# Two key parts side by side, and score pairs at other distances, in the recurrent half of a hybrid trunk

## The chip, the cores and the metric

The kernel runs on one core of a Trainium2 chip. The time is the device time of that core in microseconds (us). One of the executions is also recorded by the hardware profiler, and its record is what is called the trace here. The engines are named as in the profile: PE is TensorE (PEld its weight loads), DVE is VectorE, ACT is ScalarE, POOL is GpSimd, and SP issues transfers. L1702 is line 1702 of the kernel.

## The reference

The model is a trunk of two layers over 640 tokens (512 latent tokens and 128 context tokens) of width 1024. Layer 0 is gated attention. Layer 1 is a gated linear recurrence with 8 heads of key width 128 and value width 128, which runs over the tokens in both directions. The change touches layer 1 alone. Cut to what matters, it computes:

```python
q, f_fw, f_bw, i_in, g = split(h @ w_in)           # 5 projections of 1024 columns
q = silu(q);  v = i_in                             # per head: 128 keys, 128 values
for d in (fw, bw):
    forget = lb + (1 - lb) * sigmoid(f_d)          # the decay of one token, per key
    k      = (1 - lb) * sigmoid(-f_d)
    S_t = forget_t * S_{t-1} + k_t (outer) v_t     # from s0; backwards for bw
    o_d[t] = q_t @ S_t
o = rms_norm(o_fw + o_bw) * gain * silu(g)
out = o @ w_out                                    # then residual and layer norm
```

The outputs are both token streams, the attention's new keys and values, and the last states of the context tokens.

## The kernel before, in words

**Stages.** The attention layer and the norm behind it come first and are ordered by a planner of their own; the change leaves them alone. Then the recurrent layer goes head by head. For each head `proj_gen` computes the projections (heads 1 to 6 use a scheme of seven products for the two forget projections) and evacuates them into two tiles: `A`, which holds four parts of NT = 640 columns, and `T`, which holds the decays. The four parts of `A` are the forward keys (KF), the backward keys (KB) and the queries times their decays in either direction (QF, QB). `gla_gen` then does the recurrence of the head. All weights and activations of the projections are kept as a high and a low part, so each product is three matmuls; in the profile one line has one of the three.

**The recurrence as levels.** Inside chunks of 128 tokens the recurrence is computed as a matrix of scores. Level 0 takes neighbouring tokens, and level n takes neighbouring blocks of 2^n tokens; level 6 is the last. Each level consists of scores on PE (`scores`, L1666 to L1679) and a step `decay` (L1691): the keys of `A` are multiplied by the decays of their block (L1697 on DVE), ACT copies the keys for the next level into a tile in the right order (`kcopy`, L1647, into a tile with the tag kc or on), the decays are multiplied pairwise (L1701), and the queries of `A` are multiplied (L1702). In heads 0 to 6 the levels 1 to 6 go in pairs: both levels' keys and queries are made ready, with a copy of the queries for the lower level too (`qcopy`, L1652), and then the scores of both are asked for together. Scores are merged by DVE into one tile (L1664), or copied by ACT (L1717) and POOL (L1711). Behind the levels come `kp`, transposes of the keys (L1759) with a copy `kt` (L1761), `sp`, the products for the states of the chunks (L1765, with six updates on DVE at L1768 and L1771, two copies and two stores of the last states), `op`, the outputs (L1782 to L1785, with the sums of squares at L1790, the product with the gate at L1794 and the norm at L1797), and `oT`, their transposes (L1802). The tile of the outputs before these transposes has the tag on, the same as that of some key copies, and there is one buffer for it.

**What sets the order.** Every engine takes its instructions in one order, fixed at compile time. The program is written in an order of asking, and an instruction that has all that it needs by the compiler's own estimate can be put ahead of one asked for earlier. The order of asking is made by a small planner, `Lane` (L102). While the projections of head h + 1 are issued, each piece of them advances the lane's clock by its length in planner's units (1.28 for half a token tile of the value and gate projection, 1.6 for a group of twelve matmuls of the others). `gla_gen` of head h gives a gap with each `yield`, and its next stage is issued at the first piece at which that gap has passed (a stage that is late passes on at most SLIP = 1.0 less). A head's recurrence begins to be issued in the next projection and ends in the one behind that; a negative gap (L1798) lets the next head's recurrence be issued before this one's last stage. `lane.finish(n)` issues all that is left of the oldest heads until n are left. The projection calls it ahead of tiles that need the buffers of earlier heads (L1386, L1541). Tile dependencies, buffers and PSUM banks are held by the framework, which makes an instruction wait for those that read or write what it touches.

**The end.** Head 7 has no pairs. Its levels are issued between pieces of the output projection, whose matmuls have the name `outp`. `gate1` at L1938 takes a buffer of the tag A.

The gaps, as before:

```python
D_GLA = 5.5    # from the first key copy to level 0
D_LEV = 2.7    # a level; a pair takes 2 * D_LEV; one more ahead of kp
D_KT = 2.0     # from kp to sp
D_ST = 3.0     # from sp to op
D_OUT = 7.5    # from op to oT
```

Of the kernel before, what the change touches and what calls it, by code (L numbers as in the profile page):

```python
# [23 lines left out]
NT = TT * P  # L24
# [4 lines left out]
RH = 8  # L29
# [22 lines left out]
FORMS_AT = 3  # L52
D_GLA = 5.5
D_LEV = 2.7
D_KT = 2.0
D_ST = 3.0
D_OUT = 7.5
# [6 lines left out]
def view(t, off, dims):  # L64
    base = t[:]
    return bass.AP(base.tensor, base.offset + off, [list(base.ap[0])] + [list(d) for d in dims])
# [82 lines left out]
def hybrid_step(ctx: ExitStack, tc: tile.TileContext, a: dict, o: dict):  # L149
# [13 lines left out]
    def bank2(name, tag="b2"):  # L163
        return pools["b2"].tile([P, 2, 512], F32, tag=tag if split_banks else "b2", name=name)
# [168 lines left out]
    def gate_load(layer, eng):  # L333
        for s in range(2):
            eng.dma_start(gate[layer][:, s, :], gated[layer][s:s + 1, :].to_broadcast((P, D)))
# [981 lines left out]
            f = slice(4 * nh, 4 * nh + 4)  # L1317
            split_act(h1hi[:, f, t], h1lo[:, f, t], h[:].rearrange("p (a b) -> p a b", a=4))

    KF, QB, QF, KB = 0, NT, 2 * NT, 3 * NT  # L1320

    def wide(ps):
        return ps[:].rearrange("p a b -> p (a b)")
# [236 lines left out]
    lane = Lane()  # L1560
# [75 lines left out]
    def gla_gen(h, H):  # L1636
# [7 lines left out]
        def kcopy(w, tag="kc"):  # L1644
            nb = NT // (2 * w)
            kc = g1.tile([P, NT], F32, tag=tag, name="kc")
            nc.scalar.copy(view(kc, 0, [[2 * w, nb], [w, 2], [1, w]]), view(A, KF, [[2 * w, nb], [KB - KF + w, 2], [1, w]]))  # L1647
            return kc

        def qcopy(w):  # L1650
            nb = NT // (2 * w)
            nc.scalar.copy(view(At, 0, [[2 * w, nb], [w, 2], [1, w]]), view(A, QB, [[2 * w, nb], [QF - QB + w, 2], [1, w]]))  # L1652
            return At
# [9 lines left out]
        def merge(i, pt):  # L1663
            nc.vector.copy_predicated(blocks(near[:], 32), view(masks, i * 32, [[0, TT], [1, 32]]), blocks(pt[:, :32 * TT], 32))  # L1664

        def scores(pt, lev, kc, qc):  # L1666
            w = 1 << lev
            for c in range(TT):
                if lev < 5:
                    for b in range(4):  # L1670
                        t0 = c * P + 32 * b
                        q = qc[:, t0:t0 + 32] if qc else view(A, QB + t0, [[2 * w, 16 // w], [QF - QB + w, 2], [1, w]])
                        mm = nc.tensor.matmul(pt[32 * b:32 * b + 32, 32 * c:32 * c + 32], kc[:, t0:t0 + 32], q, start=True, stop=True)
                else:
                    for b in range(P // w):
                        ko, qo = (KB, QB) if b % 2 else (KF, QF)
                        s0, t0 = c * P + w * b, c * P + w * (b ^ 1)
                        k, q = (kc, qc) if qc else (A[:, ko:ko + NT], A[:, qo:qo + NT])
                        mm = nc.tensor.matmul(pt[w * b:w * b + w, w * c:w * c + w], k[:, s0:s0 + w], q[:, t0:t0 + w],  # L1679
                                              start=True, stop=True)  # L1680
            return mm.ins
# [9 lines left out]
        def decay(lev, keys, query=False):  # L1691
            nonlocal cur, nxt
            w = 1 << lev
            nb = NT // (2 * w)
            kc = qc = None
            kv = view(A, KF, [[KB - KF + w, 2], [2 * w, nb], [1, w]])
            nc.vector.tensor_tensor(kv, kv, view(cur, 1, [[2 * nb - 1, 2], [2, nb], [0, w]]), ALU.mult)  # L1697
            if keys:
                kc = kcopy(2 * w, keys)
            qv = view(A, QB, [[QF - QB + w, 2], [2 * w, nb], [1, w]])  # L1700
            nc.vector.tensor_tensor(view(nxt, 0, [[1, 2 * nb]]), view(cur, 0, [[2, 2 * nb]]), view(cur, 1, [[2, 2 * nb]]), ALU.mult)  # L1701
            last = nc.vector.tensor_tensor(qv, qv, view(cur, 2 * nb + 1, [[-2 * nb - 1, 2], [2, nb], [0, w]]), ALU.mult)  # L1702
            if query:
                qc = qcopy(2 * w)
            cur, nxt = nxt, cur
            return kc, qc, last

        def spread():
            for b in range(4):
                r = slice(32 * b, 32 * b + 32)  # L1710
                nc.gpsimd.tensor_copy(blocks(At[r, :], P)[:, :, r], blocks(near[r, :], 32))  # L1711

        def place(lev, pt):
            w = 1 << lev
            for b in range(P // w):
                r, o_ = slice(w * b, w * b + w), slice(w * (b ^ 1), w * (b ^ 1) + w)
                nc.scalar.copy(blocks(At[r, :], P)[:, :, o_], blocks(pt[r, :w * TT], w))  # L1717

        pairs = h < RH - 1
# [5 lines left out]
        merge(0, pt[:, 512:])  # L1725
        if pairs:
            for lev in (1, 3, 5):
                k2, _, _ = decay(lev, "on" if lev < 5 else None)
                yield 2 * D_LEV
                pt = wide(bank2("lv"))  # L1730
                late = scores(pt[:, 512:], lev + 1, k2, None)
                with tc.issue_after(late):
                    scores(pt, lev, k1, q1)
                k1, q1, last = decay(lev + 1, "kc" if lev < 5 else None, lev < 5)
                if lev < 5:
                    merge(lev, pt)
                    merge(lev + 1, pt[:, 512:])
                else:
                    spread()
                    place(5, pt)  # L1740
                    place(6, pt[:, 512:])
        else:
            for lev in range(1, 7):
                yield D_LEV
                pt = wide(bank2("lv"))
                scores(pt, lev, k1, None)
                k1, _, last = decay(lev, "kc" if lev < 4 else None)
                if lev < 5:
                    merge(lev, pt)
                else:  # L1750
                    place(lev, pt)
                if lev == 4:
                    spread()
        residual.compute(last.ins)
        yield D_LEV
        kp = bank2("kp")
        srcs = [KF + c * P for c in (0, 1, 2, 4)] + [KB + c * P for c in (1, 2, 3, 4)]
        for i, c in enumerate(srcs):
# [2 lines left out]
        nc.scalar.copy(kt, wide(kp))  # L1761
        yield D_KT
        sp = bank2("sp")
# [117 lines left out]
    for h in range(RH):  # L1881
        H = {} if h else H
        if h == RH - 1:
            sxs.close()
            side = reload_gen()
            next(side, None)
        for n, dt in enumerate(proj_gen(h, H, False) if h else first):
            lane.advance(dt)
            if h or n >= FORMS_AT:
                next(side, None)  # L1890
            if h == 0 and n == RES_AT:
                residual.compute()
                residual.loads()
        lane.add(gla_gen(h, H))
# [19 lines left out]
    def tail_steps():  # L1914
# [18 lines left out]
        for ks in ((0,), (1,), (2,), (3, 4, 5), (6,)):  # L1933
            for k in ks:
                out_k(2, k)
            yield

    gate[1] = g2.tile([P, 2, D], F32, tag="A", name="gate1")  # L1938
    gate_load(1, nc.gpsimd)
    xp = lpool("xp", 1)  # L1940
# [139 lines left out]
```

## Time and profile before

| what | value |
|---|---|
| runs | 830.49, 831.3 and 834.88 us, median 831.3 |
| profiled execution, and its span | 830.25 us, 828.4 us |
| PE, PEld busy | 793.3 us (96%), 700.5 us (85%) |
| DVE, ACT, POOL busy | 601.0 us (73%), 446.8 us (54%), 204.1 us (25%) |
| transfers | 98.12 MB, mean 118 GB/s |

Times in the trace count from the start of the span. The recurrent layer's heads with the seven products repeat with a period of about 46.5 us (L1794 of head 2 stands at 518.26, of head 3 at 564.65). Matmuls are pipelined, and their ends in the trace are modelled: a matmul normally begins before the one ahead of it has ended by the record. A matmul in full 32-bit form is two instructions. In the lists in order of time, the first two numbers are start and length in us; a bracket at the end of a row holds the idle time of the engine ahead of it and what ended that. In lists of waits the numbers are the total, how often, and the longest.

### The profile page before, as it was taken

To read this page: it belongs to the slowest core of one execution; us is meant where nothing else is said; L and a number is where in the kernel's file an instruction comes from. 1 tells how busy PE (TensorE), PEld (TensorE's weight loads), DVE (VectorE), ACT (ScalarE), POOL (GpSimd) and SP (SyncE) were. 2 spreads that over 40 slices of the span, in tenths; PEclk is the share of its full clock that TensorE was granted. 3 is DMA by queue.
4 is the path that set the end of the run, shared out by engine and by line. 5 is a ranking of instruction groups with operands and counts; after the bars stand their busy time and mean duration, and the time that the engine had idled before them with its cause. 6 is when DMAs were issued, how large, how long until landed. Compare 5 with 4: busy or idle time off the path is not lost.

```text
span 828.4 us, 19262 instructions
## 1 busy us (share of the span) xinstructions
PE 793.3 (96%) x7953; PEld 700.5 (85%) x7953; DVE 601.0 (73%) x1083; ACT 446.8 (54%) x890; POOL 204.1 (25%) x261
## 2 busy tenths in 40 slices
PE   8999999999999899999999999999999999999994
PEld 6789999888888676888998989898989989897774
DVE  4567767675777876776998795968777795868476
ACT  3252554575666775232564756657484756656242
POOL 0124001354344942101501202122212202131121
PEclk9999999999999999999999999999999999999998
DMA  9943244233140152523322342425142434235041
GB/s 326 396 168 136 102 153 154 77 128 129 51 129 26 54 176 82 198 77 94 104 94 66 106 106 69 126 70 120 46 131 66 108 96 144 84 114 169 29 156 76
DMA packets 36631, 98.12 MB, mean 118 GB/s; under 512 B 5297, under 2 KB 12481, under 8 KB 36545
## 3 DMA queue, kind: packets, MB, share of 16 engines
q1 hardware_dynamic: 25872, 78.95, 28.5%
q0 software_dynamic: 4768, 14.18, 6.1%
q10 hardware_dynamic: 5904, 3.78, 1.5%
q8 instruction: 62, 1.02, 0.5%
q14 instruction: 25, 0.20, 0.1%
HBM read 86.06 MB, written 10.83 MB: 117 GB/s over the span
## 4 chain that ended last, share of the span: by engine, by line
PE 56%; DVE 23%; ACT 10%; issue 5%; DMA 3%; POOL 2%; ACTq 0%; SPq 0%; DVEq 0%; POOLq 0%
PE pot L944 4%; PE outp L1207 4%; PE pt L1030 3%; PE outp L1209 3%; PE outp L1208 3%; DVE A L1702 3%; DVE A L1697 3%; PE rps L1445 3%; PE rps L1447 2%; PE rps L1446 2%; PE sc L917 2%; ACT kc L1647 2%; PE acc L562 2%; PE sc L918 2%; PE gps L374 2%
## 5 line engine op out<-in xcount | busy, mean ns | idle before, releaser
L1023 POOL TENSOR_SCALAR p<-p,rc 128x640 f32<-128x640 f32 x64 | 57.1, 898 | 115.3 <-DVE rc L1022 98.1
L1017 ACT ACTIVATE p<-sc,nm 128x640 f32<-128x640 f32 x64 | 51.2, 802 | 25.1 <-DVE nm L1012 15.9
L1647 ACT COPY kc<-A 128x640 f32<-128x640 f32 x47 | 37.5, 799 | 44.8 <-DVE A L1697 29.7
L1012 DVE TENSOR_REDUCE nm<-sc 128x1 f32<-128x640 f32 x64 | 51.7, 816 | 13.0 <-PE sc L918 12.8
L1711 POOL COPY At<-near 32x160 f32<-32x160 f32 x32 | 15.2, 474 | 182.4 <-PE lv L1679 160.6
L1399 PE MATMUL rps<-h1hi,rw 128*128 128x320 f32 x176 | 55.5, 316 | 0.0
L1401 PE MATMUL rps<-h1hi,rw 128*128 128x320 f32 x176 | 54.9, 312 | 0.0
L1400 PE MATMUL rps<-h1lo,rw 128*128 128x320 f32 x176 | 54.4, 309 | 0.0
L1030 PE MATMUL pt<-small,p 128*128 128x128 f32 x320 | 49.2, 279 | 2.4 <-DVE pts L922 1.2
L1377 PE MATMUL vgps<-rw,h1hi 128*128 128x512 f32 x180 | 49.0, 397 | 0.0
L1030 PEld LDWEIGHTS pt<-small,p 128*128 128x128 f32 x320 | 36.7, 141 | 11.0 <-issue 5.7
L917 PE MATMUL sc<-kk,X 128*128 128x320 f32 x128 | 43.3, 347 | 1.4 <-ACT p L1017 1.2
L922 ACT COPY pts<-pt 128x512 f32<-128x512 f32 x64 | 36.1, 590 | 15.3 <-PE pt L1030 15.2
L944 PE MATMUL pot<-pts,vv 128*64 128x256 f32 x320 | 38.3, 384 | 2.1 <-DVE pts L922 2.0
L374 PE MATMUL gps<-hhi,whi 128*128 128x320 f32 x128 | 40.0, 312 | 0.1
L1377 PE MATMUL vgps<-wspare,h1hi 128*128 128x512 f32 x140 | 39.7, 398 | 0.0
L375 PE MATMUL gps<-hlo,whi 128*128 128x320 f32 x128 | 39.6, 309 | 0.0
L376 PE MATMUL gps<-hhi,wlo 128*128 128x320 f32 x128 | 39.5, 309 | 0.0
L918 PE MATMUL sc<-klo,X 128*128 128x320 f32 x128 | 39.2, 315 | 0.0
L1377 PEld LDWEIGHTS vgps<-rw,h1hi 128*128 128x128 f32 x180 | 32.8, 188 | 7.1 <-ACT s L1510 0.4
L207 POOL TENSOR_TENSOR rstdo<-rs_t,mhalf 128x5 f32<-128x5 f32 x8 | 9.7, 1214 | 109.8 <-DVE rs_t L206 109.8
L383 PE MATMUL qmm<-whi,hhi 128*128 128x256 f32 x120 | 35.0, 292 | 0.1
(347 smaller groups left out, 2611.2 us busy)
## 6 DMA issues: line engine op xcount, KB each, us to landing
raw<-in_rec_w_in SPq DMA_DIRECT2D x40, 512.0 KB, 3.8
raw<-in_ada_m SPq DMA_DIRECT2D x16, 512.0 KB, 8.1
raw<-in_attn_w_in SPq DMA_DIRECT2D x16, 512.0 KB, 4.9
raw<-in_ada_s SPq DMA_DIRECT2D x16, 512.0 KB, 3.8
adaraw<-in_ada_c SPq DMA_DIRECT2D x11, 512.0 KB, 5.5
raw<-in_attn_w_out SPq DMA_DIRECT2D x8, 512.0 KB, 3.8
raw<-in_rec_w_out SPq DMA_DIRECT2D x8, 512.0 KB, 3.8
raw<-in_ada_c SPq DMA_DIRECT2D x5, 512.0 KB, 4.7
```

The source lines that it names most:

```text
L374: nc.tensor.matmul(ps[:, :320], w.hi(k)[:, c], hhi[:, k, t], start=(k == 0), stop=False)
L917: nc.tensor.matmul(out, X[:, h, t0:t0 + P], kk[:, c, k0:k1], start=True, stop=False)
L918: nc.tensor.matmul(out, X[:, h, t0:t0 + P], klo[:, c, k0:k1], start=False, stop=True)
L944: nc.tensor.matmul(pot[j * HD:(j + 1) * HD, :CW], vv[:, slot, c * HD:(c + 1) * HD], moving[j], start=first, stop=last)
L1012: nc.vector.tensor_reduce(nm[:, 0:1], sc[:, :, :320], AX.XY, ALU.max, negate=True)
L1023: nc.gpsimd.tensor_scalar(p, p, rs[:, 0:1], 1.0, ALU.mult, ALU.mult)
L1030: nc.tensor.transpose(pt[:, i * 256 + q * P:i * 256 + (q + 1) * P], ps[q][:, (k0 + i) * P:(k0 + i + 1) * P], ident)
L1377: nc.tensor.matmul(out, h1hi[:, k, t], wvg[i][:, k % 4].rearrange("p e n -> p (e n)"), start=(k == 0), stop=(k == KT - 1))
L1399: nc.tensor.matmul(ps[:, j, :320], hi[:, k, :], h1hi[:, k, t], start=(k == 0), stop=False)
L1400: nc.tensor.matmul(ps[:, j, :320], hi[:, k, :], h1lo[:, k, t], start=False, stop=False)
L1401: nc.tensor.matmul(ps[:, j, :320], lo[:, k, :], h1hi[:, k, t], start=False, stop=(k == KT - 1))
L1647: nc.scalar.copy(view(kc, 0, [[2 * w, nb], [w, 2], [1, w]]), view(A, KF, [[2 * w, nb], [KB - KF + w, 2], [1, w]]))
```

## The change

It has five parts, all in the recurrent layer.

1. The four parts of `A` change places: KF, KB, QB, QF at 0, 1, 2 and 3 NT instead of KF, QB, QF, KB. The step from QB to QF stays NT; that from KF to KB goes from 3 NT to NT.
2. The gap ahead of the second and the third pair goes from 5.4 to 6.0 in heads 0 to 5, and stays 5.4 in head 6.
3. Between level 0 and the first pair there are now two gaps, 2.5 and 4.5. Between them the step `decay` of level 1 is issued, which was issued together with level 0, and ahead of it `lane.finish(1)` issues what is left of the head before, which is its output transposes.
4. The gap from the third pair to `kp` goes from 2.7 to 2.0 in heads 0 to 6.
5. Behind the last projection, head 6 is issued up to its negative gap ahead of `gate1`.

```diff
+D_PAIR = 6.0
+D_LAST = 2.0
+D_TAIL = 2.5
+D_FIRST = 4.5
...
-    KF, QB, QF, KB = 0, NT, 2 * NT, 3 * NT
+    KF, KB, QB, QF = 0, NT, 2 * NT, 3 * NT
...
             for lev in (1, 3, 5):
+                if lev == 1:
+                    yield D_TAIL
+                    lane.finish(1)
                 k2, _, _ = decay(lev, "on" if lev < 5 else None)
-                yield 2 * D_LEV
+                yield D_FIRST if lev == 1 else D_PAIR if h < RH - 2 else 2 * D_LEV
                 pt = wide(bank2("lv"))
...
         residual.compute(last.ins)
-        yield D_LEV
+        yield D_LAST if pairs else D_LEV
         kp = bank2("kp")
...
+    while not lane.gens[0][2]:
+        lane.step(lane.gens[0])
     gate[1] = g2.tile([P, 2, D], F32, tag="A", name="gate1")
```

## The prediction

> **What bounds the kernel now.** I read first the busy shares of the page, then a table of stretches, then TensorE's waits, then one head in order of time. The columns of the table are busy microseconds with the number of instructions, the granted clock and the DMA share.
>
> ```profile
> PE 793.3 (96%) x7953; PEld 700.5 (85%) x7953; DVE 601.0 (73%) x1083; ACT 446.8 (54%) x890; POOL 204.1 (25%) x261
> ```
> ```profile
> 0.00:377.00 377.00, 364.16 (x2769) 310.21 (x2770) 261.04 (x515) 193.08 (x395) 111.86 (x120) 1.00 0.41 141
> ...
> 424.00:470.50 46.50, 45.92 (x613) 42.60 (x612) 36.66 (x61) 26.22 (x42) 4.79 (x8) 1.00 0.25 74
> 470.50:517.05 46.55, 45.30 (x609) 41.99 (x609) 35.40 (x60) 29.02 (x59) 10.96 (x18) 1.00 0.36 97
> 517.05:563.44 46.39, 45.16 (x609) 41.85 (x608) 35.18 (x60) 28.78 (x58) 8.50 (x14) 1.00 0.30 90
> ...
> 656.55:703.00 46.45, 45.23 (x608) 41.84 (x608) 35.23 (x60) 28.86 (x65) 10.97 (x18) 1.00 0.44 126
> 703.00:760.00 57.00, 54.91 (x801) 49.77 (x800) 44.02 (x75) 38.10 (x72) 14.23 (x21) 1.00 0.42 134
> ```
> ```profile
> PE lv L1673 <- DVE A L1702: 5.3, 14, 1.5
> PE lv L1679 <- DVE A L1702: 4.5, 6, 1.2
> PE outp L1207 <- ACT ghi L1812: 0.5, 1, 0.5
> ```
>
> The change lies behind 377 us; nothing ahead of that moves. From there to 817 us TensorE sets the time: in the head of 517.05 it is idle 46.39 - 45.16 = 1.23 us, and all its named waits between 424 and 817 us (the last fence: total, times, longest) are 10.3 us, of which 9.8 us are score matmuls `lv` that wait for the query multiply L1702. The head of 517.05 shows them in order of time:
>
> ```profile
> 519.22 0.86 PE L1377 MATMUL vgps<-wspare,h1hi 128*128 128x512 f32 x3
> 520.01 0.63 PE L1673 MATMUL lv<-A,kc 128*32 128x32 f32 x40
> ...
> 525.06 1.07 PE L1377 MATMUL vgps<-rw,h1hi 128*128 128x512 f32 x4
> ...
> 526.44 0.64 PE L1373 MATMUL vgps<-wspare,h1lo 128*128 128x256 f32 x4
> 526.92 1.09 PE L1377 MATMUL vgps<-wspare,h1hi 128*128 128x512 f32 x4
> 528.40 0.52 PE L1673 MATMUL lv<-A,kc 128*32 128x32 f32 x38 [0.39 <-DVE A L1702]
> ...
> 535.22 0.31 PE L1400 MATMUL rps<-h1lo,rw 128*128 128x320 f32 x1
> 535.71 0.53 PE L1673 MATMUL lv<-A,kc 128*32 128x32 f32 x38 [0.18 <-DVE A L1702]
> ...
> 537.66 0.31 PE L1445 MATMUL rps<-h1hi,rw 128*128 128x320 f32 x1
> ...
> 539.28 0.31 PE L1447 MATMUL rps<-h1hi,rw 128*128 128x320 f32 x1
> 540.25 0.80 PE L1679 MATMUL lv<-A 128*64 128x64 f32 x20 [0.66 <-DVE A L1702]
> 540.98 0.50 PE L1679 MATMUL lv<-At,kc 128*32 128x32 f32 x34
> ...
> 547.04 0.31 PE L1447 MATMUL rps<-thi,wspare 128*128 128x320 f32 x1
> 547.19 1.03 PE L1759 MATMUL kp<-small,A 128*128 128x128 f32 x8
> ...
> 549.83 1.95 PE L1765 MATMUL sp<-vg,kt 128*128 128x128 f32 x16
> ```
>
> Three waits a head, one ahead of each pair of levels: 0.39 + 0.18 + 0.66 = 1.23 us, the whole idle time. Their price is more than the brackets say, since a following matmul otherwise starts before the modelled end of the one before. From start to start: `kp` follows the last `rps` by 547.19 - 547.04 = 0.15 us, but pair 2 follows by 0.49 and pair 3 by 0.97, so 0.34 and 0.82 us are lost. Level 0 at 520.01 follows the third of three `vgps` (spaced 0.23, so at 519.68) by 0.33 us; pair 1 follows the fourth (527.61) by 0.79: 0.46 us. Together **1.62 us a head**.
>
> **The change, part by part.** Two paces are needed. Twelve 320-column matmuls, one step of the projection (1.6 in the planner's units), run 537.66 to 539.28 for eleven spacings: 0.147 each, 1.76 us a step. Eight `vgps` matmuls, half a token tile (1.28), run 525.06 to 526.44: 1.38 us.
>
> *Layout.* Key parts become neighbours, and so do query parts. Nothing is computed more or less; only what overlaps what changes. Before, a view over both key parts reaches from 0 to 4 NT and covers the query parts. The trace shows the order that follows:
>
> ```profile
> 525.81 0.83 DVE L1697 TENSOR_TENSOR A<-A,Tb 128x640 f32<-128x640 f32 x1 [0.35 <-ACT At L1652]
> ...
> 526.67 0.73 ACT L1647 COPY kc<-A 128x640 f32<-128x640 f32 x1 [0.41 <-DVE A L1697]
> ...
> 527.43 0.83 DVE L1702 TENSOR_TENSOR A<-A,Tb 128x640 f32<-128x640 f32 x1 [0.19 <-ACT kc L1647]
> ...
> 541.35 0.82 DVE L1697 TENSOR_TENSOR A<-A,T 128x640 f32<-128x640 f32 x1
> ```
> ```profile
> L1702 DVE TENSOR_TENSOR A<-A,T x32: 810/825/936, 431.8 to 774.3; 128x640 f32<-128x640 f32 x32
> ...
> its engine sat idle before it (us, times) until:
>   ACT kc L1647: 6.7, 15
> ```
>
> The query multiply waits for ScalarE's key copy, and the key multiply for the query copy, though neither touches the other's data. With the two ranges apart, the query multiply can follow the key multiply at once: instead of key multiply, 0.73 us copy, query multiply, the chain loses about 0.35 + 0.19 us of idle time ahead of pair 1, and the copy runs beside it. VectorE is off the path except at the three waits, so this part alone is worth what it takes off them: at least 0.19 us of the first, at most all. It also acts in the last head, which has no pairs.
>
> *Distances.* Working the due times through the planner's rule (a stage is asked for at the first yield of the projection at which it is due): level 0 stays behind the 5th yield; pair 1 goes from the 9th to the 10th, pair 2 from the 13th to the 14th, pair 3 from the 16th to the 18th (the 17th in head 6), `kp` from the 18th to the 19th, `sp` from the 19th to the 20th, `op` from the first half tile of the next projection to the third. Pair 1 thus gets 1.38 us more ahead of it against 0.46 lost. From pair 1 to pair 2 lay one half tile and three steps and now lie four steps: 1.76 - 1.38 = 0.38 us more against 0.34. From pair 2 to pair 3 it is four steps for three: 1.76 us more against 0.82. So the distances alone cover all three waits, the middle one narrowly, and there the layout adds to it. I take all three as gone.
>
> In the sum: heads 1 to 5, 5 x 1.62 = 8.1 us. Head 0 (424.00 to 470.50) is idle 46.50 - 45.92 = 0.58 us: 0.6. Head 6 (703 to 760): its pair 1 waits 1.47 us, in the row below, and 1.38 us of distance with the shorter chain covers it: 1.5. Head 7's level 1 waits 0.48 us behind a key copy of this kind (0.82 us); layout alone acts there, between 0 and 0.48: I take 0.3.
>
> ```profile
> 715.48 0.52 PE L1673 MATMUL lv<-A,kc 128*32 128x32 f32 x38 [1.47 <-DVE A L1702]
> ...
> 755.11 0.82 ACT L1647 COPY kc<-A 128x640 f32<-128x640 f32 x1 [1.02 <-DVE A L1697]
> ...
> 756.94 0.26 PE L1673 MATMUL lv<-A,kc 128*32 128x32 f32 x5 [0.48 <-DVE A L1702]
> ```
>
> Gross gain 8.1 + 0.6 + 1.5 + 0.3 = **10.5 us**.
>
> [...]
>
> *What is moved.* Three rows more of the head of 517.05 are needed:
>
> ```profile
> 533.70 1.22 DVE L1411 TENSOR_TENSOR wspare<-raw,wspare 128x1024 fp32r<-128x1024 f32 x1
> ...
> 543.56 0.49 DVE L1458 TENSOR_TENSOR u<-c,rps 128x320 f32<-128x320 f32 x1 [0.45 <-PE rps L1447]
> ...
> 548.26 1.01 ACT L1761 COPY kt<-kp 128x1024 f32<-128x1024 f32 x1 [2.45 <-PE kp L1759]
> ```
>
> `kp` now has one step behind pair 3 instead of the 5.7 us (541.48 to 547.19) of before. Behind the level-6 scores come 0.50 us of level 5 and 1.76 us of products, 2.26 us; in that time VectorE must do the key multiply (0.82 us, 0.3 us behind the end of the scores in the row of 541.35). It fits by 1.1 us unless VectorE has other work in front: 0 to 0.7 us a head. `sp` keeps its one step behind `kp`, against a copy of 1.01 us: nothing. Its six state updates, two copies and two stores on ScalarE's queue follow it and are needed by `op`, which also moves: nothing. `op` comes 2 x 1.38 us later, with its squares, the power on GpSimd, the product with the gate, and the residual's loads and stores on GpSimd's queue (25% busy). The output transposes stay behind the 7th half tile, so their slack shrinks:
>
> ```profile
> 744.13 0.28 ACT L1790 ACTIVATE kt<-op 128x128 f32<-128x128 f32 x1 [2.53 <-PE op L1782]
> ...
> 747.16 1.58 ACT L1797 ACTIVATE on<-on,rstdo 128x128 f32<-128x128 f32 x5
> ```
>
> From the first square to the scaled output this chain takes 747.16 + 1.58 - 744.13 = 4.6 us where nothing else is in its way; between `op` and the transposes now lie four half tiles (5.5 us) and level 0, so it is covered by 0.9 us and more, unless ScalarE puts other work between: 0 to 0.7 us (a key copy). The next head's first key copy and two state loads move with `op`; 2.8 us of half tiles lie between `op` and level 0: 0 to 0.6 us. In the last projection `op` of head 6 is asked for one step (1.76 us) later, and evacuation, gate and head 7's first copy stand behind it on ScalarE: 0 to 1.8 us, with output matmuls that fill TensorE; I take 0.4. *Transposes ahead of the key copy:* they are asked for at the same yield as before; the key copy into their buffer moves behind them, which it had to wait for anyhow. Cost nothing; its cover is the 4.5 that follow to pair 1. The new loop behind the last projection finds head 6 already past `op` (22nd yield of 23) and issues nothing. For all moved stages I take 0.15 us a head, 7 x 0.15 = 1.1, near the lower end since the covers above are longer than the work. Net gain 10.5 - 1.1 - 0.4 = **9.0 us**.
>
> The profiled execution took 830.25 us (a span of 828.4 and 1.85 around it), 1.05 below the median of the runs. 830.25 - 9.0 = 821.25; with the same 1.05, **822.3 us** for the median.
>
> **Rivals.** *A, the ranges are still held as one tile,* so the layout does nothing. No row of this trace tells whether ranges or whole tiles are compared; only the code, which reads and writes the four parts by slices throughout, speaks against it. Then pair 2's 0.34 us stay in five heads (1.7) and head 7's 0.3: 822.3 + 2.0 = 824.3. *B, a third or more is given back at `kp`:* VectorE has a 1.22 us weight subtraction and a 0.82 us multiply in front of the last key multiply. Then 0.15 + 1.22 + 0.82 + 0.82 - 2.26 = 0.75 us a head, 5.2 over seven: 827.5. For it: such subtractions stand between the multiplies in the rows of VectorE (73% busy); against: behind the last key multiply it sat idle 0.45 us in the row of 543.56. *C, slower:* the product's two sums of 0.5 us each, which need the step between pair 3 and `kp` to end, are issued on VectorE ahead of the last key multiply. `kp` then waits for the step's end, two sums and the multiply: 0.15 + 0.5 + 0.5 + 0.82 = 2.0 us a head, 14 over seven, against a gross 10.5: 831.3 + 3.5 = 834.8. It decides from 10.5 / 7 = 1.5 us a head. Against it: the multiply stands ahead of those sums in the program.
>
> **How the numbers follow.** The forecast gets 0.68, A 0.08, B 0.12, C 0.12. A measurement of this kernel tells about 0.5% (4.2 us) from no change. Below 827.1 us lie A, a third of B and the forecast but for 0.03, where stage costs come to their upper ends: 0.65 + 0.08 + 0.04 = 0.77 faster. Within lie these 0.03, the rest of B and 0.05 of C: 0.16. Above 835.5 lies the rest of C: 0.07. The range begins at 819.5, the gross gain with no cost and some drift, and ends at 829.0, past B; C is left out.
>
> **What would show it.** Right: no `lv` wait of TensorE for L1702 of more than 0.1 us in heads 1 to 5, periods of 44.8 to 45.1 us, no idle time of L1702 until a key copy. Wrong: those waits kept; new ones at `kp`, at the transposes `oT` or at level 0 behind its key copy; or periods that don't shrink though the waits are gone, which would mean that the idle time was only moved into spacings of the matmuls.

## The result and the profile after

The changed kernel took 826.7 us (median of nine runs, 822.66 to 830.73) against 831.3 us of the kernel before (nine runs on the same chip, 829.06 to 834.88): a ratio of 0.9938 with a 95% interval of 0.9912 to 0.9965. Measured once more on another chip it came to 0.9913 (0.9896 to 0.993). The forecast was 822.3 us. The sign was right and the time lies inside the range, but by the medians the gain is 4.6 us and not 9.0: half. The two intervals are worth 2.9 to 7.3 us and 5.8 to 8.7 us, so neither reaches the gain that was forecast.

The profiled execution took 824.67 us, with a span of 822.9. The first view is its busy shares, the second what TensorE waited for from 377 to 817 us (total, times, longest).

```profile
PE 793.2 (96%) x7953; PEld 701.2 (85%) x7953; DVE 597.8 (73%) x1083; ACT 447.8 (54%) x890; POOL 214.9 (26%) x261
```
```profile
PE lv L1677 <- ACT kc L1651: 2.7, 2, 1.8
PE outp L1212 <- issue: 0.9, 1, 0.9
PE lv L1677 <- DVE A L1706: 0.8, 1, 0.8
PE outp L1211 <- ACT ghi L1819: 0.5, 1, 0.5
PE lv L1683 <- DVE A L1706: 0.2, 1, 0.2
```

TensorE does the same work (793.2 against 793.3 us). Its 9.8 us of waits for the query multiply (L1702, now L1706) have shrunk to 1.0. But 2.7 us of waits for a key copy are new, in two places.

To see where the gain went I cut the recurrent part at the first matmul of each head's own level-0 product (`lv<-q,A`, L1688 before, L1692 after). The next views give such stretches from level 0 of one head to level 0 of the next: length, then busy time of PE, PEld, DVE, ACT and POOL with counts, granted TensorE clock (1 is full), DMA share and GB/s. The kernel after, heads 2, 5 and 6, and head 7 to the end:

```profile
518.00:562.90 44.90, 44.90 (x624) 41.75 (x612) 34.76 (x60) 29.02 (x57) 9.65 (x15) 1.00 0.31 94
...
652.70:698.60 45.90, 45.02 (x629) 41.81 (x617) 32.96 (x56) 28.05 (x51) 13.14 (x18) 1.00 0.43 126
698.60:745.60 47.00, 45.97 (x629) 42.15 (x617) 35.68 (x61) 32.20 (x70) 13.94 (x21) 1.00 0.34 106
745.60:822.90 77.30, 62.47 (x615) 51.31 (x603) 50.81 (x103) 24.15 (x66) 8.44 (x13) 0.96 0.27 98
```

and the kernel before, the same stretches:

```profile
520.50:566.80 46.30, 45.06 (x618) 41.76 (x608) 35.12 (x59) 28.73 (x57) 8.41 (x15) 1.00 0.30 91
...
659.90:705.40 45.50, 44.28 (x624) 41.20 (x613) 32.85 (x56) 27.92 (x56) 11.04 (x19) 1.00 0.44 125
705.40:752.50 47.10, 45.54 (x624) 42.12 (x612) 36.19 (x60) 31.34 (x62) 12.18 (x19) 1.00 0.39 121
752.50:828.40 75.90, 62.22 (x613) 51.22 (x600) 51.48 (x104) 25.00 (x67) 9.53 (x13) 0.95 0.25 92
```

In a middle head TensorE's idle time is gone altogether (44.90 busy in 44.90 us) and the period fell by 1.4 us. From head 5 on the kernel after is no faster: head 5 is 0.4 us longer, head 6 0.1 shorter, the last stretch 1.3 longer. The ledger, from the exact starts of those matmuls in the two profiled executions:

| stretch | before, us | after, us | difference | forecast |
|---|---|---|---|---|
| heads 0 to 4 (five periods) | 232.2 | 224.1 | -8.0 | -6.3 |
| head 5 | 45.5 | 45.9 | +0.4 | -1.5 |
| head 6 | 47.1 | 47.0 | -0.1 | -1.35 |
| head 7's level 0 to the end | 75.9 | 77.3 | +1.3 | +0.1 |
| sum | 400.7 | 394.3 | -6.4 | -9.0 |

The forecast's column takes the prediction's terms stretch by stretch (0.6 - 0.15 in head 0; 1.62 - 0.15 in each of heads 1 to 5; 1.5 - 0.15 in head 6; 0.4 - 0.3 at the end; the rounding is in the last digits).

The rows of the ledger have one flaw: level 0 doesn't stand at the same place of the projections in both kernels. The same stretches of head 0 and head 5, with the value matmuls `vgps` alone, before (the first two) and after:

```profile
427.76:474.11 46.35, 16.19 (x87) 13.23 (x87) 1.78 (x3) 0.97 (x2) 1.00 0.24 71
659.92:705.39 45.47, 14.08 (x75) 11.56 (x75) 1.79 (x3) 1.51 (x3) 1.00 0.44 125
428.62:473.02 44.40, 14.64 (x80) 12.36 (x80) 1.78 (x3) 1.56 (x3) 1.00 0.25 73
652.74:698.63 45.89, 14.88 (x80) 12.40 (x80) 1.79 (x3) 0.96 (x2) 1.00 0.43 126
```

Before, head 0's stretch holds 87 of them, head 5's 75 and head 6's 38; after, 80, 80 and 40. At the prediction's 1.38 us for eight, about 1.2 us of work left the stretches of heads 0 to 4, and about 0.9 and 0.3 us came into those of heads 5 and 6 (an estimate). With this put back, heads 0 to 4 gained about 6.8 us, head 5 0.4, and head 6 and what follows lost about 0.9 together. The sum is free of this, since all kernels have the same work ahead of head 0's level 0.

No edit of this study lies ahead of the first value matmul of all, and in the traces of the kernels before and after PE, DVE, ACT and POOL run the same instructions in the same order there. Yet in the profiled executions that matmul starts at times from 381.84 us (heads 5 and 6 with their old gaps) to 387.45 (state copies in a buffer of their own). This is why spans alone mislead here by more than the gain in question, and why stretches are compared below.

### The profile page after: what moved, and what is told of

It reads as the page before. It is cut to its first block, busy times and chain, and to the rows that moved or that the text cites. A ratio compares the mean times of both kernels' runs of the same rounds, so it can differ in the third digit from the quotient of the medians.

```text
span 822.9 us, 19277 instructions
## 1 busy us (share of the span) xinstructions
PE 793.2 (96%) x7953; PEld 701.2 (85%) x7953; DVE 597.8 (73%) x1083; ACT 447.8 (54%) x890; POOL 214.9 (26%) x261
## 4 chain that ended last, share of the span: by engine, by line
PE 78%; DVE 8%; ACT 5%; DMA 4%; issue 2%; POOL 2%; SPq 0%; ACTq 0%; DVEq 0%; POOLq 0%
PE vgps L1381 7%; PE vgps L1377 4%; PE pot L948 4%; PE outp L1211 4%; PE rps L1449 3%; PE rps L1403 3%; PE outp L1213 3%; PE outp L1212 3%; PE rps L1405 3%; PE rps L1404 3%; PE pt L1034 3%; PE rps L1451 3%; PE rps L1450 3%; PE acc L566 3%; PE lv L1677 2%
## 5 line engine op out<-in xcount | busy, mean ns | idle before, releaser
L1721 ACT COPY At<-lv 32x160 f32<-32x160 f32 (+1 forms) x48 | 15.9, 331 | 51.0 <-PE lv L1683 50.6
```

## The experiments

The table has all kernels: the ratio to the kernel before, run on the same chip, and the stretches of one profiled execution each. "Heads 0 to 4" are five periods; "head 5 on" runs from level 0 of head 5 to the end; "all" is the sum of both, and holds the same work in every kernel. Kernels with wide distances in heads 0 to 4 have the 1.2 us of value matmuls moved from the first of these columns to the second.

| kernel | ratio (95%) | heads 0 to 4, us | head 5 on, us | of that head 7 to the end | all, us |
|---|---|---|---|---|---|
| before | 1 | 232.2 | 168.5 | 75.9 | 400.7 |
| changed | 0.9938 (0.9912 to 0.9965) | 224.1 | 170.2 | 77.3 | 394.3 |
| changed, again | 0.9913 (0.9896 to 0.993) | 224.1 | 169.5 | 77.3 | 393.6 |
| layout alone | 0.9911 (0.9887 to 0.9934) | 226.6 | 165.6 | 75.3 | 392.2 |
| all but layout | 0.9924 (0.9906 to 0.9941) | 223.7 | 171.9 | 77.3 | 395.6 |
| transposes not asked for ahead | 0.993 (0.9911 to 0.9948) | 224.0 | 169.9 | 76.9 | 393.9 |
| head 6 with its old gaps | 0.9895 (0.9872 to 0.9918) | 224.0 | 167.2 | 74.5 | 391.2 |
| heads 5 and 6 with their old gaps | 0.9871 (0.9849 to 0.9893) | 224.0 | 167.2 | 75.6 | 391.2 |
| the same, old layout | 0.9886 (0.9867 to 0.9906) | 223.7 | 168.3 | 75.9 | 391.9 |
| state copies in a buffer of their own | 0.9878 (0.9857 to 0.9899) | 224.1 | 167.8 | 77.1 | 391.9 |
| head 6 with its old gaps, and that buffer | 0.9849 (0.9828 to 0.9871) | 224.1 | 166.8 | 75.1 | 390.9 |

**The layout alone.** The kernel before with one line changed.

```diff
-    KF, QB, QF, KB = 0, NT, 2 * NT, 3 * NT
+    KF, KB, QB, QF = 0, NT, 2 * NT, 3 * NT
```

> The kernel before with the new places of the four parts alone, and all gaps as before. If the distances carry the gain, the layout only shortens the chain ahead of each pair: a part of the three waits (1.23 us a head) stays, the period of heads 1 to 4 lies between 45.2 and 46.2 us, and the ratio to before is about 0.996 to 1.000. If the false order between key and query views was the cause, the waits are gone with it: periods of 44.9 to 45.0 us and a ratio of 0.991 to 0.994. If ranges are not told apart by the framework, nothing changes: 46.4 us.

It took 823.6 us against 831.0. The view of stretches shows one middle head, head 5, and the end:

```profile
562.50:607.60 45.10, 45.10 (x627) 42.05 (x616) 34.25 (x60) 28.71 (x57) 11.24 (x19) 1.00 0.34 100
...
652.70:697.00 44.30, 44.30 (x620) 41.36 (x607) 31.89 (x56) 27.81 (x56) 11.26 (x19) 1.00 0.44 130
...
743.10:818.30 75.20, 62.08 (x610) 51.08 (x598) 50.82 (x104) 24.87 (x67) 8.42 (x13) 0.95 0.26 93
```

Without any wider distance, TensorE's idle time is gone in the middle heads too. In the order of time of the same kernel the query multiply of the second level begins right behind its key multiply (no bracket, so no idle time), and it ends 4 us ahead of the scores that need it:

```profile
525.49 0.82 DVE L1697 TENSOR_TENSOR A<-A,Tb 128x640 f32<-128x640 f32 x1
526.23 0.82 DVE L1702 TENSOR_TENSOR A<-A,Tb 128x640 f32<-128x640 f32 x1
...
531.06 0.53 PE L1673 MATMUL lv<-A,kc 128*32 128x32 f32 x38
```

So the four parts of `A` are tracked by their ranges, the order that the old places forced was a false one, and lifting it is enough for most of what the middle heads had to give: 5.6 of about 6.8 us in heads 0 to 4. From head 5 on, this kernel gains 2.9 us where the changed kernel loses 1.6 (about 0.4 without the moved value matmuls). From head 0's level 0 to the end it takes 392.2 us against the changed kernel's 394.3 and 393.6. The ratios overlap, so it is not shown to be faster; but in the changed kernel nothing shows the other parts to add anything to this one line.

**All but the layout.** The changed kernel with the line above put back.

> The changed kernel with the old places of the four parts, so the gaps, the order of the transposes and the last loop alone. If the distances carry the gain: no waits of the score matmuls for the query multiply in heads 1 to 4, periods of 44.9 to 45.1 us, a ratio of 0.992 to 0.996. If the layout was the cause: the middle wait at least stays (its distance grew by only 0.38 us), periods of 45.2 to 46.2 us. The last head: if its lost 1.4 us (from its level 0 to the end) comes from the later stages of head 6, it is lost here too (77.3 us); if from the layout, it is 75.9 us as before.

It took 825.7 us. Stretches of a middle head, of head 5 and of the end:

```profile
562.50:607.30 44.80, 44.80 (x625) 41.74 (x614) 35.22 (x60) 29.29 (x57) 13.78 (x19) 1.00 0.36 100
652.10:698.70 46.60, 44.85 (x624) 41.72 (x614) 32.84 (x55) 28.23 (x51) 12.54 (x17) 1.00 0.43 124
746.70:824.00 77.30, 62.53 (x615) 51.42 (x603) 51.31 (x103) 24.16 (x66) 9.54 (x13) 0.94 0.26 98
```

The distances alone empty the middle heads of idle time as well. Here the false order is still there, as the idle time of the query multiply shows (how long, how often, until what ended), and is only covered:

```profile
  ACT kc L1651: 10.2, 14
```

Each of the two edits alone removes the same waits, so their gains don't add: 5.6 us (layout) and about 7.3 (distances) in heads 0 to 4 give about 6.8 together, the moved value matmuls put back in both. The end is as long as in the changed kernel (77.3 us), so the time lost there comes with the distances and not with the layout. The waits behind it are others, though: here the last head's scores wait for the query multiply (0.66, 1.17 and 0.97 us). No run takes the single gaps apart, nor the loop behind the last projection.

**The transposes asked for later.** The changed kernel without `lane.finish(1)` ahead of the first pair; the sum of the gaps is kept.

```diff
-                if lev == 1:
-                    yield D_TAIL
-                    lane.finish(1)
                 k2, _, _ = decay(lev, "on" if lev < 5 else None)
-                yield D_FIRST if lev == 1 else D_PAIR if h < RH - 2 else 2 * D_LEV
+                yield D_TAIL + D_FIRST if lev == 1 else D_PAIR if h < RH - 2 else 2 * D_LEV
```

> The changed kernel without the early issue of the transposes: the step of level 1 with its key copy is asked for together with level 0 again, and the distance from level 0 to the first pair is 7.0 in one piece. If the order costs nothing, as forecast: the same periods (44.9 to 45.0 us) and the same ratio as the changed kernel (0.994, within 0.002). If the order matters: pair 1 waits for a key copy that waits for the transposes, 0.3 to 1 us a head, 2 to 7 us in all.

It took 825.9 us, with the changed kernel's periods in heads 0 to 4 (44.4 and four of 44.9). This part of the change does nothing there, in either direction, as was expected. From head 5 on the two executions of the changed kernel and this one lie at 170.2, 169.5 and 169.9 us, which is no difference.

**Head 6 with its old gaps.** The changed kernel, but the gaps of head 6 (5.4, 5.4, 5.4, 2.7, no early step of level 1) are those of before.

```diff
-                if lev == 1:
+                if lev == 1 and h < RH - 2:
...
-                yield D_FIRST if lev == 1 else D_PAIR if h < RH - 2 else 2 * D_LEV
+                yield 2 * D_LEV if h == RH - 2 else D_FIRST if lev == 1 else D_PAIR
...
-        yield D_LAST if pairs else D_LEV
+        yield D_LAST if h < RH - 2 else D_LEV
```

> The changed kernel, but head 6 keeps the gaps of before in all its stages, so that its outputs are asked for one step earlier in the last projection. If the loss of 1.4 us between the level 0 of head 7 and the end comes from the later outputs of head 6, that stretch is back at 75.9 us and the time falls by about 1 to 1.5 us below the changed kernel (ratio about 0.992). If it comes from the order in which ScalarE takes weight casts and key copies in the last head, whatever head 6 does, it stays at 77.3 us.

It took 822.6 us against 831.0, and the end fell from 77.3 to 74.5 us, below the 75.9 of before, where at most a return to these had been expected. What head 6's new gaps did to the end can be read on ScalarE. First the changed kernel, whose head 7 has its level 0 at 745.6 us; the bracket is the idle time ahead of the row and what ended it:

```profile
742.75 0.97 ACT L1804 ACTIVATE on<-on,rstdo 128x128 f32<-128x128 f32 x3
...
745.25 1.03 ACT L260 CAST w<-raw 128x1024 fp32r<-128x1024 f32 x1
...
752.78 1.04 ACT L260 CAST w<-raw 128x1024 fp32r<-128x1024 f32 x1 [3.35 <-DMA raw<-in_rec_w_out]
753.73 0.72 ACT L1651 COPY kc<-A 128x640 f32<-128x640 f32 x1
```
```profile
749.29 0.39 PE L1212 MATMUL outp<-rw,ghi 128*128 128x512 f32 x1 [0.85 <-issue]
...
754.50 0.56 PE L1677 MATMUL lv<-A,kc 128*32 128x32 f32 x40 [1.82 <-ACT kc L1651]
```

The same rows with head 6's old gaps, where head 7's level 0 is at 748.2, and the one wait for a key copy in its last stretch:

```profile
742.83 1.58 ACT L1804 ACTIVATE on<-on,rstdo 128x128 f32<-128x128 f32 x5
...
752.39 1.05 ACT L260 CAST w<-raw 128x1024 fp32r<-128x1024 f32 x1 [0.86 <-DMA raw<-in_rec_w_out]
753.35 0.72 ACT L1651 COPY kc<-A 128x640 f32<-128x640 f32 x1
```
```profile
PE lv L1677 <- ACT kc L1651: 0.4, 1, 0.4
```

With the new gaps the scaling of head 6's output starts 2.9 us ahead of head 7's level 0, with the old ones 5.3. The casts of the output weights stand behind it on ScalarE, and behind a cast stands VectorE's subtraction, which reads the same buffer (L262). In the changed kernel SP's queue waited 5.1 us for such a subtraction; then the next transfer of 512 KB went out at 746.1 us and landed in 6.7, and the cast that waits for it has a key copy of head 7 behind it. This cast waits 3.35 us, the key copy comes 8.1 us behind level 0 (5.2 with the old gaps), and the scores wait 1.82 us; 0.85 us more of idle time stands at an output matmul. Together that is 2.7 us, against one such wait of 0.4 with the old gaps: 2.3 of the 2.7 us by which the two ends differ. (One output matmul more lies in the changed kernel's stretch.) That the cost comes from head 6's gaps is shown by this kernel; the way over cast and transfer is read from its rows and was not taken apart by a run of its own.

**Heads 5 and 6 with their old gaps.** As above, with `h < RH - 3` and `h > RH - 4` in place of `h < RH - 2` and `h == RH - 2`.

> The changed kernel, but heads 5 and 6 keep all gaps of before (heads 0 to 4 have the new ones, and the layout is new everywhere). If the later stages of head 5 and head 6 cause the loss in the last projection and behind it, the cycle of head 5 falls from 45.9 to about 44.3 us (no wait of level 0 of head 6 for its first key copy), and the stretch from level 0 of head 7 to the end to 74.5 to 75.2 us; with 44.9 us for heads 1 to 4 the gain is some 4 to 5 us beyond the changed kernel, a ratio of 0.987 to 0.990. If the layout's order on ScalarE causes it, head 5 or the last stretch stay where they were (45.7 and 77.3 us).

821.3 us against 832.8. The stretch of head 5:

```profile
650.50:695.90 45.40, 45.27 (x620) 42.20 (x611) 31.86 (x56) 28.06 (x57) 12.83 (x21) 1.00 0.44 126
```

TensorE is idle for 0.13 us in it, so the wait of head 6's level 0 is gone as expected; the stretch is not the 44.3 us that were expected with that, as it holds 82 value matmuls, where the layout alone had 75. From head 5 on this kernel takes 167.2 us, as with head 6 alone. Its ratio and that of the kernel before it overlap, so leaving head 5's gaps old is not shown to be worth anything beyond head 6's.

**The same with the old layout.** The last kernel with the four parts in their old places.

> The same gaps as the run before it, with the old places of the four parts. If the distances are enough for themselves in heads 0 to 4: periods of 44.8 us there; heads 5 and 6, with old gaps and the old layout, are as before the change (45.5 and 47.1 us, the last stretch 75.9). Ratio about 0.991. What lies between this run and the one before it is then the layout's worth where the gaps are old, some 2 to 3 us.

823.1 us. Heads 0 to 4 are as with the new layout (223.7 against 224.0), and from head 5 on it is 1.1 us longer, where 2 to 3 us had been expected. The ratios overlap. Where the distances cover the waits, the layout is worth nothing more; the 1.1 us would be that of the heads without wide distances.

**The changed kernel again**, on the chip of the last two.

> The changed kernel as it is, on the chip of the two runs before it, for a comparison beside them: ratio 0.992 to 0.996, head cycles and last stretch as in its first profile (44.9 us for heads 1 to 4, 45.9 for head 5, 77.3 to the end).

824.75 us against 832.77. Heads 0 to 4 took 224.1 us again; head 5 took 45.2 us here and 45.9 in the first profile, so the loss there varies from one execution to the next.

**State copies in a buffer of their own.** TensorE's idle time that is left in head 5 was still to be explained. In the changed kernel TensorE waits for the first key copy of head 6, and this copy for a DMA, a store of the last states. In order of time, SP's and ACT's queues among the rows:

```profile
687.32 2.22 SPq L1624 DMA_DIRECT2D glo<-gd  x5
...
688.92 0.43 ACT L1782 COPY ns<-sp 128x128 f32<-128x128 f32 x2 [0.31 <-DVE S L1778]
689.22 0.89 ACTq L1783 DMA_DIRECT2D out_new_s<-ns  x2
...
697.13 1.00 ACT L1651 COPY kc<-A 128x640 f32<-128x640 f32 x1 [2.91 <-DMA out_new_s<-ns]
...
698.19 0.63 PE L1677 MATMUL lv<-A,kc 128*32 128x32 f32 x40 [0.88 <-ACT kc L1651]
```

The copy `ns` of the last states has the tag kc: it lies in the buffer of the key copies, so the next key copy must wait until the two stores have read it. In the kernel before they were issued beside the first of five reloads of spilled tiles on SP's queue. The first store landed in 1.6 us and the second, 0.08 us behind the first reload, in 3.4 (the list has the median, 2.5):

```profile
694.02 0.43 ACT L1775 COPY ns<-sp 128x128 f32<-128x128 f32 x2
694.31 0.94 ACTq L1776 DMA_DIRECT2D out_new_s<-ns  x2
694.67 2.26 SPq L1620 DMA_DIRECT2D glo<-gd  x5
...
out_new_s<-ns ACTq DMA_DIRECT2D x2, 64.0 KB, 2.5
```

With `sp` one step later they come 1.9 us behind the start of those reloads, and land after 7.2 us (the list of DMA issues from 685 to 700 us: KB each, median us to landing):

```profile
glo<-gd SPq DMA_DIRECT2D x5, 320.0 KB, 7.1
...
out_new_s<-ns ACTq DMA_DIRECT2D x2, 64.0 KB, 7.2
```

So a store of 64 KB took as long here as the reloads of 320 KB each, 1.6 MB together, that went out just ahead of it (6.9 and 7.4 us against a median of 7.1). Head 6's two stores in the same kernel, with none of these reloads ahead of them, landed in 2.1 us (median). No run tells whether the late ones landed only behind the reloads or merely shared something with them. If the buffer is the cause, one of its own for `ns` must remove the wait with everything else kept:

```diff
-        ns = g1.tile([P, 2, P], F32, tag="kc", name="ns")
+        ns = g1.tile([P, 2, P], F32, tag="ns", name="ns")
```

> The changed kernel, but the copy of the last states (ns) has a buffer of its own instead of the one of the key copies (tag kc). If the 0.9 us wait of head 6's level 0 comes from the store of head 5's states, which is now issued behind the six reloads of the spilled heads and holds that buffer until it lands, then the key copy no longer waits for a transfer, the wait is gone, the cycle of head 5 is 45.0 us and the time from level 0 of head 0 to the end 393 us (394.3 and 393.8 with the shared buffer); heads 1 to 4 and the last stretch stay (44.9 and 77.3 us). If the key copy is late for another reason (ScalarE's order), the wait of 0.3 to 0.9 us stays.

822.7 us against 832.3. Heads 5 and 6 and the end:

```profile
656.00:700.90 44.90, 44.90 (x623) 41.74 (x612) 33.58 (x58) 29.32 (x57) 13.51 (x18) 1.00 0.44 131
700.90:746.70 45.80, 45.65 (x629) 42.22 (x617) 34.55 (x59) 30.90 (x62) 12.90 (x21) 1.00 0.34 110
746.70:823.80 77.10, 62.47 (x612) 51.29 (x599) 50.65 (x103) 24.10 (x66) 8.42 (x13) 0.95 0.25 97
```
```profile
out_new_s<-ns ACTq DMA_DIRECT2D x2, 64.0 KB, 7.3
```

The store is as slow as before (7.3 us) and nobody waits for it: head 5's period is the 44.9 us of the heads ahead of it. Head 6 is 1.2 us shorter too: its pair 1 no longer waits for 0.78 us (the 0.8 for L1706 among the waits of the changed kernel), and from 650 to 748 us this kernel has no wait of TensorE at all. The end stays at 77.1. With the new gaps in head 6, the shared buffer is thus shown to be the cause of these two waits, and not of the loss at the end.

**Both remedies.** Head 6 with its old gaps, and the buffer of its own.

> The same own buffer together with the old gaps for head 6. If both losses are separate: head 5's cycle 45.0 us, the last stretch 74.5 us, and 390 to 390.5 us from level 0 of head 0 to the end; a ratio of 0.986 to 0.989. If the store only hid another wait, head 5's cycle stays at 45.7 us and the sum at 391.2 us.

820.4 us against 832.3, the lowest ratio of the study, 1.5% below the kernel before (the intervals of the three kernels above it in the table overlap with its own). By the stretches it is ahead of the changed kernel by 3.4 us, or 2.8 against that one's second execution (390.9 against 394.3 and 393.6 from head 0's level 0 on):

```profile
652.40:697.30 44.90, 44.90 (x624) 41.74 (x611) 33.68 (x59) 29.40 (x57) 13.60 (x18) 1.00 0.44 131
...
744.10:819.10 75.00, 62.10 (x610) 51.09 (x597) 50.71 (x103) 24.84 (x67) 8.43 (x13) 0.95 0.25 93
```

Its end is 2.1 us shorter than with the buffer alone, so the price of head 6's new gaps was seen twice, at 2.7 and 2.1 us. The two remedies overlap: head 6's old gaps gave 3.1 us alone and the buffer 2.4, but behind the first the buffer adds only 0.3, which is not clear of the scatter. In head 6, pair 1 now waits 0.98 us for a key copy.

Against the kernel before the stretches gain 9.8 us. With the value matmuls put back, heads 0 to 5 bring about 8.3 of them, where the prediction had 7.8, so there the waits were worth what it said; head 6 brings about 0.7 instead of 1.35, and the end 0.9 instead of a loss of 0.1.

## Why the prediction was right and wrong

**Right: the place and the price of the waits.** "Together 1.62 us a head", less 0.15 for moved stages, against a measured 1.5 in heads 1 to 4 (46.33 to 46.57 before, 44.93 after). The periods are in the 44.8 to 45.1 that were named, and the query multiply no longer sits idle until a key copy. Single heads saved 1.4 to 1.6 us, more than the 1.23 us of the brackets, so a wait did cost more than its idle time, as the distances from start to start had it. Head 0's stretch got 1.9 us shorter and not 0.6 because seven value matmuls, about 1.2 us, left it. In the kernel before, level 0 of heads 1 to 5 stood behind the 47th of the 80 value matmuls of the projection beside it, now behind the 40th. The prediction had level 0 stay where it was; why it moved in the compiled order stays open.

**Right: "the distances alone cover all three waits".** The kernel with the old layout shows it, idle time none. The layout's price, "at least 0.19 us of the first, at most all", was true but far too wide: the bound was worked out for one wait, and the false order stood in front of all three. It removed all three. Rival A fell with that. That the two edits remove the same thing, the prediction had only half said ("there the layout adds to it"); in heads 0 to 4 it adds nothing.

**Right: the transposes cost nothing; `kp` has room.** There is no wait of TensorE at `kp` in the changed kernel, so rivals B and C did not come about. In the head behind 562.9 us the last key multiply is done in time, as the order of time shows:

```profile
588.12 0.80 PE L1683 MATMUL lv<-A 128*64 128x64 f32 x20
588.96 0.83 DVE L1701 TENSOR_TENSOR A<-A,T 128x640 f32<-128x640 f32 x1 [0.25 <-PE lv L1683]
...
591.20 1.03 PE L1766 MATMUL kp<-small,A 128*128 128x128 f32 x8
```

It starts 0.04 us behind the end of the level-6 scores (588.12 + 0.80), and `kp` follows 1.4 us behind its end, with no bracket.

Elsewhere one of the signs that the prediction named for "wrong" did appear: a wait at level 0 behind its key copy, 0.88 us in head 6. The next two points have its cause and the other new wait.

**Wrong: "Its six state updates, two copies and two stores on ScalarE's queue follow it and are needed by `op`, which also moves: nothing."** The step asked who needs the data of the moved stores, but not who needs the buffer that they read, nor what they are moved past. They hold the key copies' buffer, and one step later they stand behind the reloads on SP's queue (6.9 and 7.4 us to landing, where it was 1.6 and 3.4). TensorE's idle time in head 5's stretch fell only from 1.22 to 0.88 us, where all of it should have gone, so with the five value matmuls more put back it gained 0.4 us where 1.5 was forecast. The run with a buffer of its own is 1.0 us shorter there (0.3 against the second execution) and 1.2 in head 6.

**Wrong: "`op` of head 6 is asked for one step (1.76 us) later ... 0 to 1.8 us ... I take 0.4."** The engine was the right one, ScalarE, and the upper bound was still too low. It counted the delay itself, not what is next behind it: the casts of the output weights, the transfers that wait for their buffers, and a key copy of the last head. Measured by head 6's old gaps, the end costs 2.1 to 2.7 us more. It shows as only +1.3 in the ledger since the last head itself got faster by the layout, by more than the 0.3 of the forecast: alone, the layout makes the last stretch 0.7 us shorter (75.9 to 75.3). The waits for L1702 there were two, of 0.48 and 1.2 us (the longest of the row of L1679 in the prediction's list of waits), and only the first was counted.

**Wrong in size: head 6's 1.5 us.** The wait of 1.47 ahead of its pair 1 only halved, to 0.78, and its period fell by 0.1. With the store out of the way the wait is gone and the period 1.3 shorter than before, so with the new gaps this too is the buffer's doing. The forecast's other reason, the shorter chain, was sufficient alone: with the layout alone, old gaps and the shared buffer, no score matmul of head 6 waits.

Two overlooked costs thus make the miss, the store's buffer and the casts behind `op`. With the moved value matmuls put back, heads 0 to 4 brought about 6.8 us (6.3 were forecast), and from head 5 on about 0.4 was lost where 2.7 should have been won. That the time came out inside the range is in part luck: the range was drawn for costs at `kp`, which did not come about, and it was wide enough for the two others.

## What to carry to other kernels

When a stage is moved, follow its stores too: ask which buffer each of them holds, who is next to write that buffer, and what is issued on other queues between the old place and the new. Two edits that remove the same wait do not add, so measure each alone; look for the false order first (two parts that nobody shares, spanned by one view), since lifting it costs no distance anywhere. Distances that suit the middle of a loop are to be looked at again for its last turns, where the work behind them is another. And a period cut at an instruction that itself moves has moved work in it: count what lies between the marks before the difference is read.

## What the runs showed of the hardware

Of two stores of 64 KB, issued on ACT's queue, one landed in 1.6 us ahead of 1.6 MB of reloads on SP's queue and one in 3.4 us behind the first 320 KB of them (the kernel before); behind all five, the two took 6.9 and 7.4 us (the changed kernel, where ScalarE sat idle for 2.91 us ahead of the next key copy until they had landed). In the kernel whose key copies don't share their buffer they took 7.3 us (median), and no key copy waited for them. And single executions of the same instructions differ by 5.6 us at 380 us into the kernel (381.84 and 387.45), while heads 0 to 4 behind them take 224.1 us in three executions, two of the changed kernel and the one with that buffer. For a change of one per cent, stretches of the trace show here what spans do not.
